# Encoder trunk on one core: x's two parts in one 512-column matmul, a new PSUM layout, and vectors fetched at other times

## The chip, the core and the metric

The kernel runs on one core of a Trainium2 chip. Its time is the device time of one execution in microseconds; a comparison uses the median over rounds. Engines are named as in the profile: PE is TensorE (PEld its weight loads), DVE is VectorE, ACT is ScalarE, POOL is GpSimd, and SP issues the DMAs.

## What is computed

Two layers work on x, 256 tokens of 1024 features in float32. Each layer has three steps, every one followed by a layer norm of `ALPHA*x + step`:

```python
x = layer_norm(ALPHA * x + 0.5 * swiglu(x, ffn1...))      # 1024 -> 2816 -> 1024
proj = x @ w_in                                             # u | gate_b | gate_c | h | q | k | v
y = concat(pool_mixer(u), gated_conv(gate_b, gate_c, h), neighbourhood_attention(q, k, v, rpb)) @ w_out
x = layer_norm(ALPHA * x + y)
x = layer_norm(ALPHA * x + 0.5 * swiglu(x, ffn2...))
# swiglu(x) = (silu(x @ w_gate) * (x @ w_up)) @ w_down
```

Attention has 8 heads of 64 columns on a grid of 4 rows by 64 columns, with a bias per head that is read from a small table, and a mask that keeps a query to 16 key columns.

## The kernel before

**Products.** Every operand is split exactly into a high and a low part that the matmul takes at full rate (`hi` is a cast on ACT, `lo = raw - hi` on DVE). A product is three matmuls: x's high part by the weight's high part, x's low part by the weight's high part, x's high part by the weight's low part.

**Weights.** Weights come in units of 512 KB by DMAs on SP's queue into four raw buffers. ACT (line 178) and DVE (line 179) split each unit into one of twelve pairs of slots. A unit is issued when a place is free, one per `pc.step`.

**Three ways of multiplying.** `x_stat` (lines 290 to 292) has x stationary and 512 weight columns moving: the first 512 gate and up columns, and v and u|gate_b. `w_stat` (lines 303 to 305) has 128 weight columns stationary and x's 256 tokens moving, so that its result comes out transposed: 256 columns of the weights make one group of two column tiles (`ft`) by eight chunks of the features (`kc`) by three matmuls. There are 36 pairs of such groups (gate and up) in the four feed-forward parts, and six groups (q0, k0, q1, k1, gate_c, h) in each mixer part. `r_stat` (lines 315 to 317) has transposed activations stationary and 512 columns of the down or output weights moving.

**PSUM.** Eight banks in two pools: four one-bank buffers `acc` for the accumulators (two token tiles by two halves) and the attention scores, four one-bank buffers `mm` for all else.

**Order of the work.** All five engines run their instructions in the order in which the program issues them. That order is set by the `Pacer`. Its clock advances with the matmuls issued (`MM512`, `MM256`); `pc.at(delay, ...)` puts a piece of work off until the first `pc.step` at which the clock has advanced by `delay`, and `pc.need(tag)` runs what is left of a tag. A step first runs the work that is due and then issues at most one weight unit. A `w_stat` group has four blocks of four `kc`, with a step after each of the first three and one more after the group's evacuation.

**Mixers.** After v and u|gate_b come q0, k0, q1, k1, gate_c, h, and then the output projection. The attention of four heads (`a0` from q0 and k0, `a1` from q1 and k1) goes in two calls of `attention`, two heads each, and four stages: `scores` (PE; DVE adds the bias and takes the maximum; ACT the exponentials), `normalise` (DVE, line 712), `transposed` (PE, line 721; ACT copies), `weighted` (PE, line 735; ACT and DVE write the output's two parts, lines 748 and 749). The delays between them are `A_S`, `A_NORM`, `A_TR`, `A_PV`. The convolution (`conv_mixer`, lines 662 to 668) follows the product h.

**Other vectors.** `load_gb` fetches the layer norm's two vectors, spread over the partitions, `GB_AT` after the part before has ended. `load_bias` fetches a bias (four DMAs, lines 572 and following) and adds the mask on POOL (line 579). The layer norm's `rs = (var + eps)^-0.5` is two POOL instructions (lines 342 and 343).

Of the kernel before, what the change touches and what calls it, by code (L numbers as in the profile page):

```python
# [16 lines left out]
P = 128  # L17
SEQ = 256
# [28 lines left out]
# units of the weights that go before the second token tile at the start, and where its transposes stand  # L47
X1_AT = 4
X1_TR = 3
# how long after its operands were ordered a step is issued, in microseconds of the tensor engine's work  # L50
LN_TR = (4.5, 7.2)
GB_AT = 14.0
# [5 lines left out]
A_NORM = 2.6  # L58
A_TR = 1.2
A_PV = 1.4  # L60
# about how long a product of the tensor engine takes: these pace the work of the other engines
MM512 = 0.218
MM256 = 0.1095


class Pacer:
    """Places work of the other engines, and the next weights, between groups of matrix products."""
# [53 lines left out]
def encoder_kernel(  # L121
# [18 lines left out]
    ps_acc = ctx.enter_context(tc.tile_pool(name="ps_acc", bufs=4, space=PSUM))  # L140
    ps_mm = ctx.enter_context(tc.tile_pool(name="ps_mm", bufs=4, space=PSUM))
# [14 lines left out]
    def mirrored(v):  # L156
        """The same view, its last axis run backwards."""
        dims = [list(d) for d in v.ap]
        step, n = dims[-1]
        dims[-1] = [-step, n]  # L160
        return bass.AP(tensor=v.tensor, offset=v.offset + (n - 1) * step, ap=dims)
# [4 lines left out]
    def bank(tag="mm"):  # L166
        pool = ps_mm if tag == "mm" else ps_acc
        return pool.tile([P, 512], F32, tag=tag, name=nm(tag))

# [88 lines left out]
    def new_xT():  # L258
        hi = xp.tile([P, KC, SEQ], F32R, tag="xhi", name=nm("xhi"))
        lo = xp.tile([P, KC, SEQ], F32R, tag="xlo", name=nm("xlo"))  # L260
        return hi, lo
# [32 lines left out]
    def w_stat(ps, key, xT):  # L294
        """256 columns of the weights against all tokens, transposed out."""
        for ft in range(2):
            c = slice(ft * P, (ft + 1) * P)
            for i in range(2):
                hi, lo = pc.get((*key, i))
                for j in range(4):  # L300
                    kc = i * 4 + j
                    o = ps[:, ft * SEQ : (ft + 1) * SEQ]
                    PE.matmul(o, hi[:, j, c], xT[0][:, kc, :], start=(kc == 0), stop=False)  # L303
                    PE.matmul(o, hi[:, j, c], xT[1][:, kc, :], start=False, stop=False)  # L304
                    PE.matmul(o, lo[:, j, c], xT[0][:, kc, :], start=False, stop=(kc == KC - 1))  # L305
                if ft == 1:
                    pc.free((*key, i))
                if ft == 0 or i == 0:
                    pc.step(12 * MM256)

    def r_stat(ps, key, act, t, n, first, last):
        """A chunk of transposed activations against half a row unit."""
        hi, lo = pc.get(key)
        ts = slice(t * P, (t + 1) * P)
        PE.matmul(ps, act[0][:, ts], hi[:, n, :], start=first, stop=False)  # L315
        PE.matmul(ps, act[1][:, ts], hi[:, n, :], start=False, stop=False)  # L316
        PE.matmul(ps, act[0][:, ts], lo[:, n, :], start=False, stop=last)  # L317

# [17 lines left out]
    def ln_rest(t, stats, store):  # L336
        g, b = gbs[-1]
        xt = xs[t]
        mv = sp.tile([P, 2], F32, tag="mv", name=nm("mv"))
        rs = sp.tile([P, 1], F32, tag="rs", name=nm("rs"))  # L340
        DVE.bn_aggr(mv, stats.rearrange("p a b -> p (a b)"))  # L341
        POOL.tensor_scalar(rs, mv[:, 1:2], EPS, None, ALU.add)  # L342
        POOL.tensor_tensor(rs, rs, half_t, ALU.pow)
        for h in range(2):
            DVE.scalar_tensor_tensor(xt[:, hs[h]], xt[:, hs[h]], mv[:, 0:1], g[:, hs[h]], ALU.subtract, ALU.mult)
        for c in hs:
            DVE.scalar_tensor_tensor(xt[:, c], xt[:, c], rs[:, 0:1], b[:, c], ALU.mult, ALU.add)
            if store:
                SP.dma_start(out[0, t * P : (t + 1) * P, c], xt[:, c])

    def finish(keys, act, acc, last_key, next_gb, store, stop):
        """The last products into acc, one token tile after the other, and the layer norm."""
        nT = None if store else new_xT()
        for t in range(NT):
            stats = sp.tile([P, 2, 6], F32, tag="stats", name=nm("stats"))
            # the first half of the columns is done early where something waits for the layer norm
# [42 lines left out]
    def ffn(key, xT, next_gb, stop, store=False):  # L399
# [17 lines left out]
        # first four column tiles with the token tiles apart  # L417
        gk, uk = (*key, "g", 0), (*key, "u", 0)
        if key == (0, 0):
# [9 lines left out]
            for k in (gk, uk):  # L429
                ps = [bank() for _ in range(NT)]  # L430
# [16 lines left out]
        else:  # L447
            for t in range(NT):
                pc.need(f"x{t}")
                gate = bank()  # L450
                x_stat(gate, gk, 512, t, xT, t == 1)
                sg = silu(gate)
                pc.step(6 * MM512)
                up = bank()
                x_stat(up, uk, 512, t, xT, t == 1)
                gated_transposed(t, (sg,), up)
                pc.step(6 * MM512)
# [6 lines left out]

        for p in range(2, NPAIR):
            gate = bank()
            w_stat(gate, (*key, "g", p), xT)
            sg = silu(gate)
            pc.step(12 * MM256)
            up = bank()  # L470
            w_stat(up, (*key, "u", p), xT)
            hT = hts[p] = new_h()
            hf = gated(up, sg).rearrange("p (a b) -> p a b", a=2)
            ACT.copy(hT[:, 0], hf)  # L474
            DVE.tensor_tensor(hT[:, 1], hf, f32(hT[:, 0]), ALU.subtract)
            pc.step(12 * MM256)
            pc.need("h")
            # the down projection runs behind
# [15 lines left out]
    consts = {}  # L494

    def setup():
# [8 lines left out]
        # additive mask of a query column block: its rows run with the column falling  # L505
# [38 lines left out]
        pc.at(30, "cw", columns)  # L544
        # the bias table, each line in the middle of a longer one
# [12 lines left out]
        # probabilities: the columns out of a block's reach stay zero  # L558
# [9 lines left out]
    def load_bias(l, q):  # L568
        n = 4 * ROWS
        rv = bp.tile([P, n, WIN], F32, tag="rbias", name=nm("rbias"))  # L570
        for r in range(ROWS):
            SP.dma_start(
                rv[r * QB : (r + 1) * QB, :, :],
                dram(consts["tabs"][r], (l * HEADS + 4 * q) * ROWS * TABW, [[1, QB], [TABW, n], [1, WIN]]),
            )
        bias = bp.tile([P, 2, n, KW], F32, tag="bias", name=nm("bias"))
# [6 lines left out]
        return bias  # L583

    def mixers(l, xT, next_gb, stop):
# [12 lines left out]
        biases = {0: load_bias(l, 0)}  # L598
# [31 lines left out]
        for t in range(NT):  # L630
            pc.need(f"x{t}")
            pv = bank()
# [3 lines left out]
            pu = bank()  # L636
# [16 lines left out]
        def proj(name):  # L653
            ps = bank()
            w_stat(ps, (*key, name), xT)
            return ps.rearrange("p (a b) -> p a b", a=2)
# [13 lines left out]
        def attention(j, qT, kT, q):  # L670
            """Two heads, in the upper and the lower half of the rows: one stage after the other."""
# [81 lines left out]
        def qk(q):  # L753
            pq = proj(f"q{q}")
            qT = hp.tile([P, 2, 2, P], F32, tag="qk", bufs=4, name=nm("qT"))
            for j in range(2):
                for b in range(2):
                    src = mirrored(pq[:, j, :].rearrange("p (r c) -> p r c", c=GRID)[:, :, b * QB : (b + 1) * QB])
                    ACT.mul(qT[:, j, b, :].rearrange("p (r c) -> p r c", c=QB), src, HD ** -0.5)
            pc.step(12 * MM256)  # L760
            pk = proj(f"k{q}")
            kT = hp.tile([P, 2, SEQ], F32, tag="qk", bufs=4, name=nm("kT"))
            ACT.copy(kT, pk)
# [4 lines left out]
            pc.step(12 * MM256)  # L768

        qk(0)  # L770
        pc.at(A_S + A_STEP + 2, "bias1", lambda: biases.update({1: load_bias(l, 1)}))
# [3 lines left out]
        ACT.copy(gc, p_)  # L775
        pc.step(12 * MM256)
        p_ = proj("h")
        z = ap_.tile([P, 2, SEQ + 2], F32, tag="a", name=nm("z"))
        POOL.memset(z[:, :, 0:1], 0.0)
        POOL.memset(z[:, :, SEQ + 1 :], 0.0)  # L780
        DVE.tensor_tensor(z[:, :, 1 : SEQ + 1], p_, gc, ALU.mult)
        conv_mixer(z)
        pc.step(12 * MM256)
# [8 lines left out]
        pc.need("ya")  # L792
        pc.need("a0")
# [9 lines left out]
        pc.need("a1")  # L803
# [42 lines left out]
```

## Time and profile before

| what | value |
|---|---|
| runs | 979.34, 980.66, 981.9 us; median 980.66 |
| profiled execution, span from first to last instruction | 979.4 us (no other time is given for it) |
| PE busy | 950.6 us, 97%, 6201 matmuls |
| PEld busy | 865.1 us, 88% |
| DVE busy | 580.3 us, 59% |
| ACT busy | 437.7 us, 45% |
| POOL busy | 65.6 us, 7% |
| moved by DMA | 178.95 MB, mean 183 GB/s |

A row of the profile's groups gives line, engine, operation, output and inputs, the count, the busy time with the mean of one instruction, and the idle time of the engine before them with what ended it. Timeline rows start with the time in the span and the duration. Matmuls overlap each other, so a matmul's duration is longer than the step from one start to the next, and a "busy" PE can still be slowed; the steps are what counts.

### The profile page before, as it was taken

What the parts mean: (1) busy time and instruction counts of PE and PEld (TensorE: products, weight loads), DVE (VectorE), ACT (ScalarE), POOL (GpSimd) and SP (SyncE); (2) the same over time, 40 slices, a digit from 0 to 9 for tenths busy, and PEclk for the clock granted to TensorE, in tenths of its full rate; (3) what the DMA queues carried; (4) which work ended last, traced back from release to release, by engine and by line L of the source; (5) the groups of instructions that cost most, each with busy time, mean ns of one, the idle gap of its engine ahead of it and who ended that gap; (6) DMA issues with size and microseconds to landing.
All of it is one profiled execution on the core that took longest, in us unless ns stands there. A gap on an engine that the chain in (4) does not pass through costs nothing.

```text
span 979.4 us, 15259 instructions
## 1 busy us (share of the span) xinstructions
PE 950.6 (97%) x6201; PEld 865.1 (88%) x6201; DVE 580.3 (59%) x670; ACT 437.7 (45%) x585; POOL 65.6 (7%) x118
## 2 busy tenths in 40 slices
PE   7999999998999999999999999999889999999996
PEld 5999999878888999999888999998688889999995
DVE  5755544676768644545676454548676776454525
ACT  6544434335734534434344444443465354344410
POOL 4000000024101000000000000002050000000001
PEclk9999999999999999999999999999989999999999
DMA  8887665568345866565468556664754377556601
GB/s 287 277 264 216 190 194 173 145 185 241 106 129 169 258 194 188 175 195 177 135 211 254 176 172 194 191 186 110 252 153 123 109 229 243 177 174 193 192 23 43
DMA packets 129077, 178.95 MB, mean 183 GB/s; under 512 B 14752, under 2 KB 100848, under 8 KB 129008
## 3 DMA queue, kind: packets, MB, share of 16 engines
q1 hardware_dynamic: 129008, 177.99, 59.3%
q8 instruction: 48, 0.79, 0.3%
q14 instruction: 21, 0.17, 0.0%
HBM read 176.84 MB, written 1.13 MB: 182 GB/s over the span
## 4 chain that ended last, share of the span: by engine, by line
PE 83%; DVE 7%; DMA 5%; issue 2%; ACT 1%; POOL 1%; SPq 1%; POOLq 0%; DVEq 0%; ACTq 0%
PE mm L303 16%; PE mm L304 16%; PE mm L305 16%; PE acc L315 9%; PE acc L316 9%; PE acc L317 9%; DMA raw<-in_w_in_dram 3%; DVE wlo L179 2%; PE mm L292 2%; PE mm L290 2%; PE mm L291 2%; ACT whi L178 1%; PE mm L721 1%; DMA raw<-in_ffn_w_down_dram 1%; DMA raw<-in_ffn_w_up_dram 1%
## 5 line engine op out<-in xcount | busy, mean ns | idle before, releaser
L179 DVE TENSOR_TENSOR wlo<-raw,whi 128x1024 fp32r<-128x1024 f32 (+1 forms) x321 | 390.0, 1231 | 303.1 <-ACT whi L178 302.0
L178 ACT CAST whi<-raw 128x1024 fp32r<-128x1024 f32 (+1 forms) x321 | 331.1, 1045 | 328.9 <-issue 131.2
L303 PE MATMUL mm<-xhi,whi 128*128 128x256 f32 x1344 | 384.0, 286 | 0.0
L304 PE MATMUL mm<-xlo,whi 128*128 128x256 f32 x1344 | 382.0, 284 | 0.0
L305 PE MATMUL mm<-xhi,wlo 128*128 128x256 f32 x1344 | 381.8, 284 | 0.0
L303 PEld LDWEIGHTS mm<-xhi,whi 128*128 128x128 f32 x1344 | 259.7, 193 | 3.0 <-issue 1.5
L304 PEld LDWEIGHTS mm<-xlo,whi 128*128 128x128 f32 x1344 | 259.6, 193 | 1.4
L305 PEld LDWEIGHTS mm<-xhi,wlo 128*128 128x128 f32 x1344 | 259.5, 193 | 0.0
L315 PE MATMUL acc<-whi,hT 128*128 128x512 f32 x352 | 137.9, 392 | 0.0
L316 PE MATMUL acc<-whi,hT 128*128 128x512 f32 x352 | 137.4, 390 | 0.0
L317 PE MATMUL acc<-wlo,hT 128*128 128x512 f32 x352 | 137.0, 389 | 0.0
L317 PEld LDWEIGHTS acc<-wlo,hT 128*128 128x128 f32 x352 | 66.1, 188 | 14.0
L291 PE MATMUL mm<-whi,xlo 128*128 128x512 f32 x192 | 75.3, 392 | 2.9 <-DVE xlo L271 2.9
L315 PEld LDWEIGHTS acc<-whi,hT 128*128 128x128 f32 x352 | 66.2, 188 | 12.7
L316 PEld LDWEIGHTS acc<-whi,hT 128*128 128x128 f32 x352 | 66.2, 188 | 12.3
L290 PE MATMUL mm<-whi,xhi 128*128 128x512 f32 x192 | 76.7, 399 | 0.4 <-ACT whi L178 0.4
L292 PE MATMUL mm<-wlo,xhi 128*128 128x512 f32 x192 | 75.2, 392 | 0.5 <-DVE wlo L179 0.5
L342 POOL TENSOR_SCALAR rs<-mv 128x1 f32<-128x1 f32 x12 | 9.4, 780 | 847.0 <-DVE mv L341 847.0
L474 ACT CAST hT<-hf 128x512 fp32r<-128x512 f32 x36 | 22.3, 620 | 75.2 <-DVE hf L396 75.2
L291 PEld LDWEIGHTS mm<-whi,xlo 128*128 128x128 f32 x192 | 36.4, 189 | 10.8 <-DVE xlo L271 3.8
L292 PEld LDWEIGHTS mm<-wlo,xhi 128*128 128x128 f32 x192 | 36.2, 188 | 8.9 <-DVE wlo L179 1.3
L290 PEld LDWEIGHTS mm<-whi,xhi 128*128 128x128 f32 x192 | 36.3, 189 | 8.2 <-ACT whi L178 1.3
(93 smaller groups left out, 556.9 us busy)
## 6 DMA issues: line engine op xcount, KB each, us to landing
raw<-in_ffn_w_up_dram SPq DMA_DIRECT2D x88, 512.0 KB, 4.7
raw<-in_ffn_w_down_dram SPq DMA_DIRECT2D x88, 512.0 KB, 4.1
raw<-in_ffn_w_gate_dram SPq DMA_DIRECT2D x87, 512.0 KB, 4.1
raw<-in_w_in_dram SPq DMA_DIRECT2D x40, 512.0 KB, 4.7
raw<-in_w_out_dram SPq DMA_DIRECT2D x16, 512.0 KB, 4.8
lng<-in_ln_g_dram SPq DMA_DIRECT2D x6, 512.0 KB, 6.8
lnb<-in_ln_b_dram SPq DMA_DIRECT2D x6, 512.0 KB, 8.3
rbias<-tab SPq DMA_DIRECT2D x16, 96.0 KB, 5.1
```

The source lines that it names most:

```text
L178: ACT.copy(hi, raw)
L179: DVE.tensor_tensor(lo, raw, f32(hi), ALU.subtract)
L290: PE.matmul(ps, xT[0][:, kc, ts], hi[:, j, :], start=(kc == 0), stop=False)
L291: PE.matmul(ps, xT[1][:, kc, ts], hi[:, j, :], start=False, stop=False)
L292: PE.matmul(ps, xT[0][:, kc, ts], lo[:, j, :], start=False, stop=(kc == KC - 1))
L303: PE.matmul(o, hi[:, j, c], xT[0][:, kc, :], start=(kc == 0), stop=False)
L304: PE.matmul(o, hi[:, j, c], xT[1][:, kc, :], start=False, stop=False)
L305: PE.matmul(o, lo[:, j, c], xT[0][:, kc, :], start=False, stop=(kc == KC - 1))
L315: PE.matmul(ps, act[0][:, ts], hi[:, n, :], start=first, stop=False)
L316: PE.matmul(ps, act[1][:, ts], hi[:, n, :], start=False, stop=False)
L317: PE.matmul(ps, act[0][:, ts], lo[:, n, :], start=False, stop=last)
L474: ACT.copy(hT[:, 0], hf)
```

## The change

- `xT` becomes one tile with both parts of x. In `w_stat` the two matmuls with the weight's high part become one with 512 moving columns (two runs of 256: high part, low part). Its result fills one bank: the first half takes the products with x's high part, the second those with x's low part. The third matmul adds into the first half.
- After each `w_stat` group, ACT copies the second half out of PSUM (`lower`), and DVE adds it to the first. Silu, the halving of up, and the product of the two then work on SBUF.
- PSUM: two buffers `mm` of two banks each, for `w_stat` and `x_stat`; four one-bank buffers `acc` for all else (accumulators, scores, transposes, attention output, pooling product).
- `GB_AT` is 45 rather than 14. The first bias of a mixer part is fetched and masked in the feed-forward part before (at pair 6), and the second is fetched there too and masked at `BIAS_AT`.
- `rs`'s addition of eps is a DVE instruction.
- `A_NORM` is 3.6 rather than 2.6, `A_TR` 2.2 rather than 1.2. `a1` is completed before the output projection rather than after its first two keys. The transpose of the convolution's taps comes in the first mixer part.
- Comments go.

```diff
-GB_AT = 14.0
+GB_AT = 45.0
-A_NORM = 2.6
-A_TR = 1.2
+A_NORM = 3.6
+A_TR = 2.2
+BIAS_AT = A_S + A_STEP + 3.0
-MM256 = 0.1095
+MM768 = 0.347
...
-    ps_acc = ctx.enter_context(tc.tile_pool(name="ps_acc", bufs=4, space=PSUM))
-    ps_mm = ctx.enter_context(tc.tile_pool(name="ps_mm", bufs=4, space=PSUM))
+    ps_one = ctx.enter_context(tc.tile_pool(name="ps_one", bufs=4, space=PSUM))
+    ps_two = ctx.enter_context(tc.tile_pool(name="ps_two", bufs=2, space=PSUM))
...
+    def bank(tag="acc"):
+        return ps_one.tile([P, 512], F32, tag="acc", name=nm(tag))
+    def banks():
+        return ps_two.tile([P, 2, 2, SEQ], F32, tag="mm", name=nm("mm"))
...
-        hi = xp.tile([P, KC, SEQ], F32R, tag="xhi", name=nm("xhi"))
-        lo = xp.tile([P, KC, SEQ], F32R, tag="xlo", name=nm("xlo"))
-        return hi, lo
+        both = xp.tile([P, 2, KC, SEQ], F32R, tag="xT", name=nm("xT"))
+        return both[:, 0], both[:, 1], both
...
-                    PE.matmul(o, hi[:, j, c], xT[0][:, kc, :], start=(kc == 0), stop=False)
-                    PE.matmul(o, hi[:, j, c], xT[1][:, kc, :], start=False, stop=False)
-                    PE.matmul(o, lo[:, j, c], xT[0][:, kc, :], start=False, stop=(kc == KC - 1))
+                    PE.matmul(ps[:, ft], hi[:, j, c], xT[2][:, :, kc, :], start=(kc == 0), stop=False, ...)
+                    PE.matmul(ps[:, ft, 0], lo[:, j, c], xT[0][:, kc, :], start=False, stop=(kc == KC - 1), ...)
...
+    def lower(ps, scale=1.0):
+        t = tp.tile([P, 2, SEQ], F32, tag="t", name=nm("lw"))
+        ACT.activation(t, ps[:, :, 1], AF.Copy, scale=scale)
+        return t
...
-        POOL.tensor_scalar(rs, mv[:, 1:2], EPS, None, ALU.add)
+        DVE.tensor_scalar(rs, mv[:, 1:2], EPS, None, ALU.add)
...
+        def bias_ahead():
+            ahead["bias"] = {0: add_mask(fetch_bias(key[0], 0))}
+            ahead["rv"] = fetch_bias(key[0], 1)
+            if key[1] == 0 and p == 6:
+                pc.at(0, "bias", bias_ahead)
...
-            gate = bank()
+            gate = banks()
             w_stat(gate, (*key, "g", p), xT)
-            sg = silu(gate)
-            pc.step(12 * MM256)
-            up = bank()
+            sg = lower(gate)
+            DVE.tensor_tensor(sg, gate[:, :, 0], sg, ALU.add)
+            ACT.activation(sg, sg, AF.Silu)
+            pc.step(4 * MM768)
+            up = banks()
             w_stat(up, (*key, "u", p), xT)
             hT = hts[p] = new_h()
-            hf = gated(up, sg).rearrange("p (a b) -> p a b", a=2)
+            hf = lower(up, 0.5)
+            DVE.scalar_tensor_tensor(hf, up[:, :, 0], 0.5, hf, ALU.mult, ALU.add)
+            DVE.tensor_tensor(hf, hf, sg, ALU.mult)
...
             pq = proj(f"q{q}")
+            ql = lower(pq, HD ** -0.5)
+            DVE.scalar_tensor_tensor(ql, pq[:, :, 0], HD ** -0.5, ql, ALU.mult, ALU.add)
-                    ACT.mul(qT..., src, HD ** -0.5)      # src from PSUM
+                    ACT.copy(qT..., src)                  # src from ql
...
-            ACT.copy(kT, pk)
+            kl = lower(pk)
+            DVE.tensor_tensor(kT, pk[:, :, 0], kl, ALU.add)
...
-        pc.at(A_S + A_STEP + 2, "bias1", lambda: biases.update({1: load_bias(l, 1)}))
+        pc.at(BIAS_AT, "bias1", lambda: biases.update({1: add_mask(rv1)}))
...
-        ACT.copy(gc, p_)
+        gl = lower(p_)
+        DVE.tensor_tensor(gc, p_[:, :, 0], gl, ALU.add)
...
-        DVE.tensor_tensor(z[:, :, 1 : SEQ + 1], p_, gc, ALU.mult)
+        hl = lower(p_)
+        DVE.tensor_tensor(hl, p_[:, :, 0], hl, ALU.add)
+        DVE.tensor_tensor(z[:, :, 1 : SEQ + 1], hl, gc, ALU.mult)
         conv_mixer(z)
...
-        pc.need("ya")
-        pc.need("a0")
+        for tag in ("ya", "a0", "a1"):
+            pc.need(tag)
         for k in keys[:2]:
...
-        pc.need("a1")
         return finish(keys[2:], act, acc, keys[-1], next_gb, False, stop)
```

More of the change, by code (lines that the diff above doesn't have):

```diff
@@ L164, in halves, with apart @@
         return [slice(i * n // 2, (i + 1) * n // 2) for i in range(2)]
-    def bank(tag="mm"):
-        pool = ps_mm if tag == "mm" else ps_acc
-        return pool.tile([P, 512], F32, tag=tag, name=nm(tag))
+    def bank(tag="acc"):
+        return ps_one.tile([P, 512], F32, tag="acc", name=nm(tag))
+    def banks():
+        return ps_two.tile([P, 2, 2, SEQ], F32, tag="mm", name=nm("mm"))
+    def apart(two):
+        return two.rearrange("p a b c -> p a (b c)")
     def unit_tiles(shape):
@@ L301, in w_stat @@
                     kc = i * 4 + j
[L302 to L305, printed above, removed]
+                    PE.matmul(
+                        ps[:, ft], hi[:, j, c], xT[2][:, :, kc, :],
+                        start=(kc == 0), stop=False, skip_group_check=True,
+                    )
+                    PE.matmul(
+                        ps[:, ft, 0], lo[:, j, c], xT[0][:, kc, :],
+                        start=False, stop=(kc == KC - 1), skip_group_check=True,
+                    )
                 if ft == 1:
@@ L428, in ffn @@
             res = []
-            for k in (gk, uk):
-                ps = [bank() for _ in range(NT)]
+            both = [apart(banks()) for _ in range(NT)]
+            for which, k in enumerate((gk, uk)):
+                ps = [b[:, which] for b in both]
                 seq = [(i, t) for i in range(4) for t in range(NT)]
@@ L449, in ffn @@
                 pc.need(f"x{t}")
-                gate = bank()
+                both = apart(banks())
+                gate, up = both[:, 0], both[:, 1]
                 x_stat(gate, gk, 512, t, xT, t == 1)
@@ L463, in act @@
             return [hts[f // 2][:, i, f % 2, :] for i in range(2)]
+        def bias_ahead():
+            ahead["bias"] = {0: add_mask(fetch_bias(key[0], 0))}
+            ahead["rv"] = fetch_bias(key[0], 1)
         for p in range(2, NPAIR):
-            gate = bank()
+            if key[1] == 0 and p == 6:
+                pc.at(0, "bias", bias_ahead)
+            gate = banks()
             w_stat(gate, (*key, "g", p), xT)
-            sg = silu(gate)
-            pc.step(12 * MM256)
-            up = bank()
+            sg = lower(gate)
+            DVE.tensor_tensor(sg, gate[:, :, 0], sg, ALU.add)
+            ACT.activation(sg, sg, AF.Silu)
+            pc.step(4 * MM768)
+            up = banks()
             w_stat(up, (*key, "u", p), xT)
             hT = hts[p] = new_h()
-            hf = gated(up, sg).rearrange("p (a b) -> p a b", a=2)
+            hf = lower(up, 0.5)
+            DVE.scalar_tensor_tensor(hf, up[:, :, 0], 0.5, hf, ALU.mult, ALU.add)
+            DVE.tensor_tensor(hf, hf, sg, ALU.mult)
             ACT.copy(hT[:, 0], hf)
             DVE.tensor_tensor(hT[:, 1], hf, f32(hT[:, 0]), ALU.subtract)
-            pc.step(12 * MM256)
+            pc.step(4 * MM768)
             pc.need("h")
@@ L542, in columns @@
             DVE.tensor_copy(cw, trp)
-        pc.at(30, "cw", columns)
+        consts["columns"] = columns
         tab = ap_.tile([P, 7 * TABW], F32, tag="a", name="tab")
@@ L565, in setup, with fetch_bias @@
         consts.update(icnt=icnt, mask=mask, pw=pw, cw=cw, tabs=tabs)
-    def load_bias(l, q):
+    def fetch_bias(l, q):
         n = 4 * ROWS
@@ L575, in load_bias, with add_mask @@
             )
+        return rv
+    def add_mask(rv):
+        n = 4 * ROWS
         bias = bp.tile([P, 2, n, KW], F32, tag="bias", name=nm("bias"))
@@ L583, in load_bias @@
         return bias
+    ahead = {}
     def mixers(l, xT, next_gb, stop):
@@ L597, in mixers @@
         POOL.memset(U[:, :, PADL + SEQ :], 0.0)
-        biases = {0: load_bias(l, 0)}
+        biases, rv1 = dict(ahead.pop("bias")), ahead.pop("rv")
+        if l == 0:
+            pc.at(POOL_AT - 4, "cw", consts["columns"])
         def pool_means():
@@ L631, in mixers @@
             pc.need(f"x{t}")
-            pv = bank()
+            both = apart(banks())
+            pv, pu = both[:, 0], both[:, 1]
             x_stat(pv, (*key, "v"), 512, t, xT, t == 1)
@@ L635, in mixers @@
             pc.step(6 * MM512)
-            pu = bank()
             x_stat(pu, (*key, "ug"), 512, t, xT, t == 1)
@@ L653, in proj @@
         def proj(name):
-            ps = bank()
+            ps = banks()
             w_stat(ps, (*key, name), xT)
-            return ps.rearrange("p (a b) -> p a b", a=2)
+            return ps
         def conv_mixer(z):
@@ L754, in qk @@
             pq = proj(f"q{q}")
+            ql = lower(pq, HD ** -0.5)
             qT = hp.tile([P, 2, 2, P], F32, tag="qk", bufs=4, name=nm("qT"))
+            DVE.scalar_tensor_tensor(ql, pq[:, :, 0], HD ** -0.5, ql, ALU.mult, ALU.add)
             for j in range(2):
                 for b in range(2):
-                    src = mirrored(pq[:, j, :].rearrange("p (r c) -> p r c", c=GRID)[:, :, b * QB : (b + 1) * QB])
-                    ACT.mul(qT[:, j, b, :].rearrange("p (r c) -> p r c", c=QB), src, HD ** -0.5)
-            pc.step(12 * MM256)
+                    src = mirrored(ql[:, j, :].rearrange("p (r c) -> p r c", c=GRID)[:, :, b * QB : (b + 1) * QB])
+                    ACT.copy(qT[:, j, b, :].rearrange("p (r c) -> p r c", c=QB), src)
+            pc.step(4 * MM768)
             pk = proj(f"k{q}")
             kT = hp.tile([P, 2, SEQ], F32, tag="qk", bufs=4, name=nm("kT"))
-            ACT.copy(kT, pk)
+            kl = lower(pk)
+            DVE.tensor_tensor(kT, pk[:, :, 0], kl, ALU.add)
             first = attention(0, qT, kT, q)
@@ L767, in qk @@
             pc.at(A_S + A_STEP, f"a{q}", second)
-            pc.step(12 * MM256)
+            pc.step(4 * MM768)
         qk(0)
-        pc.at(A_S + A_STEP + 2, "bias1", lambda: biases.update({1: load_bias(l, 1)}))
+        pc.at(BIAS_AT, "bias1", lambda: biases.update({1: add_mask(rv1)}))
         qk(1)
@@ L774, in mixers @@
         gc = ap_.tile([P, 2, SEQ], F32, tag="a", name=nm("gc"))
-        ACT.copy(gc, p_)
-        pc.step(12 * MM256)
+        gl = lower(p_)
+        DVE.tensor_tensor(gc, p_[:, :, 0], gl, ALU.add)
+        pc.step(4 * MM768)
         p_ = proj("h")
+        hl = lower(p_)
         z = ap_.tile([P, 2, SEQ + 2], F32, tag="a", name=nm("z"))
@@ L780, in mixers @@
         POOL.memset(z[:, :, SEQ + 1 :], 0.0)
-        DVE.tensor_tensor(z[:, :, 1 : SEQ + 1], p_, gc, ALU.mult)
+        DVE.tensor_tensor(hl, p_[:, :, 0], hl, ALU.add)
+        DVE.tensor_tensor(z[:, :, 1 : SEQ + 1], hl, gc, ALU.mult)
         conv_mixer(z)
-        pc.step(12 * MM256)
+        pc.step(4 * MM768)
         acc = [[None, None], [None, None]]
```

## The prediction

> **What bounds the kernel now.** I read the share of each engine, the groups by line, PE's timeline, and then the waits around PE's idle stretches. PE is busy 97% of the span, and lines 303 to 305 hold the largest part:
>
> ```profile
> PE 950.6 (97%) x6201; PEld 865.1 (88%) x6201; DVE 580.3 (59%) x670; ACT 437.7 (45%) x585; POOL 65.6 (7%) x118
> PE mm L303 16%; PE mm L304 16%; PE mm L305 16%; PE acc L315 9%; PE acc L316 9%; PE acc L317 9%; DMA raw<-in_w_in_dram 3%; DVE wlo L179 2%; PE mm L292 2%; PE mm L290 2%; PE mm L291 2%; ACT whi L178 1%; PE mm L721 1%; DMA raw<-in_ffn_w_down_dram 1%; DMA raw<-in_ffn_w_up_dram 1%
> ...
> L303 PE MATMUL mm<-xhi,whi 128*128 128x256 f32 x1344 | 384.0, 286 | 0.0
> ```
>
> What counts is the step from start to start:
>
> ```profile
> 101.19 0.28 PE L305 MATMUL mm<-xhi,wlo 128*128 128x256 f32 x1
> 101.31 0.40 PE L315 MATMUL acc<-whi,hT 128*128 128x512 f32 x1
> ...
> 106.55 0.39 PE L317 MATMUL acc<-wlo,hT 128*128 128x512 f32 x1
> 106.77 0.28 PE L303 MATMUL mm<-xhi,whi 128*128 128x256 f32 x1
> ...
> 242.97 0.28 PE L303 MATMUL mm<-xhi,whi 128*128 128x256 f32 x1
> ...
> 246.56 0.28 PE L303 MATMUL mm<-xhi,whi 128*128 128x256 f32 x1
> ```
>
> Between the two 512-column ends lie 24 matmuls: (106.77 - 101.31) / 24 = 0.2275 us each, the last of them followed by a 256-column one (0.22). The last two rows are ten triples of 256 columns apart: 0.359 us a triple, 0.120 a matmul, also where a 512-column one follows (101.19 to 101.31). So 512 columns cost less than two times 256: about 13 ns per matmul do not depend on the columns.
>
> PE's idle time lies mostly in the two mixer parts:
>
> ```profile
> 202.43 4.10 DVE L347 SCALAR_TENSOR_TENSOR x<-x,rs,lnb 128x512 f32<-128x512 f32 x2 [0.47 <-POOL rs L343]
> 202.46 3.52 POOL L579 TENSOR_TENSOR bias<-rbias,mask 128x640 f32<-128x640 f32 x2
> 295.26 1.42 DVE L347 SCALAR_TENSOR_TENSOR x<-x,rs,lnb 128x512 f32<-128x512 f32 x2 [0.46 <-POOL rs L343]
> 211.73 0.50 PE L291 MATMUL mm<-whi,xlo 128*128 128x512 f32 x1 [1.47 <-DVE xlo L271]
> 209.25 0.50 SPq L325 DMA_DIRECT2D lng<-in_ln_g_dram  x1
> 220.09 1.05 ACT L178 CAST whi<-raw 128x1024 fp32r<-128x1024 f32 x1 [4.19 <-DMA raw<-in_w_in_dram]
> 227.76 1.11 PE L644 MATMUL mm<-ident,un 128*128 128x128 f32 x4 [3.17 <-ACT un L639]
> 707.73 0.66 PE L644 MATMUL mm<-ident,un 128*128 128x128 f32 x4 [3.05 <-ACT un L639]
> 228.00:232.00 4.00, 4.00 (x24) 4.00 (x24) 2.04 (x3) 1.32 (x2) 2.22 (x2) 0.64 0.85 312
> 708.00:712.00 4.00, 4.00 (x24) 4.00 (x23) 2.01 (x3) 1.32 (x2) 1.37 (x1) 0.59 0.91 334
> 247.96 0.30 PE L721 MATMUL mm<-ident,pz 128*128 128x128 f32 x1 [0.87 <-DVE pz L712]
> 249.44 1.79 PE L721 MATMUL mm<-ident,pz 128*128 128x128 f32 x11 [1.18 <-DVE pz L712]
> 728.56 0.30 PE L721 MATMUL mm<-ident,pz 128*128 128x128 f32 x1 [1.39 <-DVE pz L712]
> 730.04 2.18 PE L721 MATMUL mm<-ident,pz 128*128 128x128 f32 x9 [1.18 <-DVE pz L712]
> 731.00:736.00 5.00, 5.00 (x25) 5.00 (x24) 2.79 (x7) 3.29 (x5) 0.00 (x0) 0.50 0.36 102
> ```
>
> In order: a layer norm's DVE step took 2.05 us while POOL masked a bias, 0.71 without, and PE waited 1.47 for the x behind it; the layer norm vectors went out ahead of weights, ACT waited 4.19 us for a weight, and PE over 3 us for ACT's copy behind it; PE waited for the softmax. In the three windows the last but two numbers show the granted clock: 0.5 to 0.64 after idle stretches of some 3 us.
>
> **The change, part by part.**
>
> *The merged matmul.* A triple (0.359) becomes 0.2275 + 0.120 = 0.3475. By 1344: 15.5 us; with the steps that follow one another without rounding (0.360 against 0.347) 17.5. I take **-17**. No row has a moving operand in two runs; the bounds are one matmul (0.2275) and two (0.240), the second giving nothing. I take the first, since both runs are of 256 contiguous columns.
>
> The Trainium skill's page "TensorE: Matmul & The Clock Gate" (section "Back-to-back issue gap") gives N/2.4 + 2.5 ns for a gap: by it the triple would go from 327 to 325 ns, and the change would save 3.4 us. The trace's 120 and 227.5 ns contradict so small a fixed part.
>
> *The evacuation.* Per group one ACT copy and one DVE addition more (84 groups), and for up a DVE product; 0.59 and 0.69 us each by the rows below. Gate: copy, addition, silu end some 2.5 us after the group, and its two banks are needed again after up's 5.6 us. hT's chain (0.6 + 2 x 0.69 + 0.62 + 0.69) meets its use one pair later. **Nothing** there; without that cover it would be 84 x 1.6 = 134 us. In the mixers it does not stay free (below).
>
> *Vectors fetched elsewhere.* The wait for un goes (6.2 us in both parts; I keep 0.5 each for the weights' own rate): **-5.2**, and the slowed clock after it, 4 x 0.36 + 4 x 0.41 = **-3.1**. The bias mask no longer lies on the layer norm: **-3.0** (1.47 twice). What is moved: two 512 KB DMAs to 45 us, among weights that have twelve places of lead; and in the feed-forward part two fetches of a bias, the second of which holds SP until POOL has masked the first (5.1 us landing and two masks of 1.7 each, 8.5 us). SP normally waits for buffers, so weights late by that much cost ACT a wait, not PE: 0, at most 2 us a layer.
>
> *eps on DVE.* Layer norms wait 0.46 for POOL less; only the last one ends the kernel: **-0.3**. The taps' transpose: 0.
>
> *The softmax.* The waits before (0.87 + 1.18 + 1.39 + 1.18) go, **-4.6**, and half the clock in five to six us, **-3.0**. In their place comes the new order. Rows for it:
>
> ```profile
> rbias<-tab SPq DMA_DIRECT2D x16, 96.0 KB, 5.1
> L396 DVE SCALAR_TENSOR_TENSOR hf<-mm,sg 128x512 f32<-128x512 f32 x44 | 30.0, 685 | 13.7 <-PE mm L305 12.5 <-PE mm L292 1.2
> L391 ACT ACTIVATE sg<-mm 128x512 f32<-128x512 f32 x44 | 26.2, 597 | 21.5 <-PE mm L305 18.3 <-PE mm L292 3.2
> L712 DVE TENSOR_SCALAR pz<-pz,sm 128x160 f32<-128x160 f32 x32 | 12.6, 435 | 0.6
> 241.23 1.36 PE L686 MATMUL acc<-kT,qT 64*128 64x160 f32 x16
> 242.84 0.48 DVE L695 TENSOR_TENSOR Sb<-acc,bias 128x320 f32<-128x320 f32 x1
> 248.44 0.18 ACT L700 ACTIVATION_READ_ACCUMULATOR pz<-Sb,mx 128x1 f32 x1
> L721 PE MATMUL mm<-ident,pz x16: 272/279/329, 267.6 to 269.9; 128*128 128x128 f32 x16
> L735 PE MATMUL mm<-PT,v x16: 379/379/430, 273.0 to 274.6; 128*64 128x256 f32 x16
> ```
>
> A step is now 4 x 0.347 = 1.39 us, so the stages fall on steps 2, 5, 7 and 9 after k is ordered (they fell on 2, 4, 5 and 7). On step 5 `normalise` stands behind a weight's split and, for a0, behind q1's addition. Let K be the end of k0's matmuls: 239.8 before (scores at 241.23 follow a block of 1.4 later). The bias addition started at K + 3.0 and the exponentials ended at K + 8.8. With kT's addition: K + 9.4. Then cast 1.05, split 1.23, addition 0.69, and four heads' scaling at 0.63 each: first head ready at K + 13.0, last at 14.9. PE reaches the transposes at K + 6 x 1.39 + 1.36 = 9.7, idles 3.3, and ends at 15.4 instead of 12.1: **+3.3**. For a1, k1's addition, the output of a0 and a split hold the bias addition until K + 5.2; the same chain gives the first head at 13.4, the last at 15.3. PE arrives at K + 1.8 + 1.36 + 8.3 = 11.5: **+1.9**.
>
> *The output projection.* a1's `weighted` falls on step 9, which comes behind `conv_mixer` on ACT and DVE, and its two results take two of the four `acc` banks, which the third and fourth accumulator need.
>
> ```profile
> 274.14 0.27 ACT L748 CAST yT<-mm 128x128 fp32r<-128x128 f32 x1 [1.84 <-PE mm L735]
> ...
> 275.92 0.29 DVE L749 TENSOR_TENSOR yT<-mm,yT 128x128 fp32r<-128x128 f32 x1 [0.33 <-ACT yT L748]
> ...
> 277.87 0.40 PE L315 MATMUL acc<-whi,yT 128*128 128x512 f32 x1
> ...
> 278.73 0.68 DVE L781 TENSOR_TENSOR z<-mm,gc 128x512 f32<-128x512 f32 x1
> ...
> 283.04 0.62 ACT L667 CAST yT<-cs 128x512 fp32r<-128x512 f32 x1 [5.49 <-DVE cs L665]
> ```
>
> h ended at E = 277.9; z came 0.85 later, the cast of y 4.3 after z. With h's addition the cast ends at E + 0.85 + 0.69 + 4.3 + 0.62 = 6.45, DVE's low part at 7.2, and the first result's four readings (a pair of results took 274.14 to 276.21) at 8.1. PE has issued `weighted` (1.8) and two accumulators (6 x 0.2275) by E + 3.15: **+4.95**. Bounds: 0 if the banks were free, 6.4 if the fourth accumulator waits as long.
>
> *Clock.* An idle 5 us costs some 3.4 us at half speed, 1.7, in both parts; the transposes' idle 3.3 does so more often than not, the 1.9 rarely: **+6** in all.
>
> *Sum:* -17 - 5.2 - 3.1 - 3.0 - 0.3 - 4.6 - 3.0 = -36.2; 2 x (3.3 + 1.9 + 4.95) + 6 = +26.3; together -9.9 on a span of 979.4. The median is 980.66, 1.3 above the span: **971 us**.
>
> **Rivals.**
>
> *Two runs cost two matmuls.* Place: every w_stat triple. At 0.240 instead of 0.2275 the -17 is gone: 988, slower. It decides from 9.5 ns on (12.8 us / 1344). For: no such operand in the trace. Against: nothing else in a matmul's step depends on where its columns lie in these rows. 6%. The skill page's formula would, in this sum, give 985; the rows speak against it: 3%.
>
> *The evacuation beside POOL.* Where POOL works, DVE took 2.05 for 0.71; the convolution's 4.3 us so slowed is 12, and the wait at the output projection 8 longer in both parts: 987. It decides from 6.4 a part. POOL has only short work there: 7%.
>
> *The banks are free.* If a1's results are read before the accumulators want them, 9.9 and their clock go: 958. Against: the order just counted. 20%. If the softmax is hidden too, 945: 6%.
>
> *Gains and new waits cancel* (each new wait 1 to 2 us longer): 978 to 983.6, 13%.
>
> **How the numbers follow.** The forecast (962 to 977.7) has 45%. Range 951 to 986: it leaves out 945, 987 and 988 (0.19). About 0.3%, 2.9 us, can be told from no change: faster 0.45 + 0.20 + 0.06 = 0.71, same 0.13, slower 0.06 + 0.03 + 0.07 = 0.16.
>
> **What would show it.** Line 303's successor at steps of 0.227 and 0.120; no wait for un and none of L291 for xlo in the mixers; the transposes of pz waiting for DVE some 3 and 2 us; the third accumulator of the output projection 5 us late behind yT, the granted clock low after it. Wrong if the 512-column step is 0.24, or if PE runs through the mixers without these waits.

## The result, and the profile after

The changed kernel takes 998.63 us (997.76 to 999.25) against 981.28 before, a ratio of 1.018 with an interval of 1.0165 to 1.0198: slower by some 17 us, where 971 was forecast. The page of the profiled execution (999.25 us, span 997.5):

```profile
span 997.5 us, 12731 instructions
PE 952.5 (95%) x4857; PEld 794.7 (80%) x4857; DVE 629.5 (63%) x766; ACT 484.5 (49%) x663; POOL 58.5 (6%) x106
...
L308 PE MATMUL mm<-xT,whi 128*128 128x512 f32 x1344 | 479.9, 401 | 4.8 <-DVE hf L412 4.8
L312 PE MATMUL mm<-xT,wlo 128*128 128x256 f32 x1344 | 378.0, 281 | 0.0
L296 PE MATMUL mm<-whi,xT 128*128 128x512 f32 x192 | 80.1, 417 | 12.0 <-ACT sg L407 8.9
```

PE runs 1344 matmuls fewer than before and is busy for longer. Line 296 (the first matmul of `x_stat`, line 290 before) has 12 us of idle time in front of it; it had 0.4. PE's list of waits (engine and line, what it waited for, us in total, times, longest) says the same of the whole kernel (some rows):

```profile
PE acc L331 <- DVE yT L784: 9.3, 2, 4.6
PE mm L296 <- ACT sg L407: 8.9, 6, 2.0
...
PE mm L308 <- DVE hf L412: 4.8, 1, 4.8
PE acc L756 <- DVE pz L747: 4.6, 4, 1.4
PE mm L296 <- ACT v L670: 2.7, 4, 0.7
PE acc L721 <- DVE kT L801: 1.1, 2, 0.5
...
PE acc L679 <- ACT un L674: 0.4, 1, 0.4
```

and of the kernel before:

```profile
PE mm L644 <- ACT un L639: 6.2, 2, 3.2
...
PE mm L721 <- DVE pz L712: 4.6, 4, 1.4
PE mm L291 <- DVE xlo L271: 2.9, 2, 1.5
```

The waits for un and xlo are gone, as forecast, and the output projection's wait (first row) has come, as forecast. The rows for sg, v and hf were not forecast: 16.4 us. Timeline rows and two windows of them (the window's last three numbers are the granted clock, DMA's share and GB/s):

```profile
39.39 0.63 PE L308 MATMUL mm<-xT,whi 128*128 128x512 f32 x1 [4.75 <-DVE hf L412]
318.70 0.50 PE L296 MATMUL mm<-whi,xT 128*128 128x512 f32 x1 [2.03 <-ACT sg L407]
...
39.50:43.00 3.50, 3.50 (x11) 2.95 (x12) 2.70 (x3) 1.96 (x3) 0.00 (x0) 0.51 0.92 315
319.50:322.90 3.40, 3.40 (x9) 2.64 (x8) 1.44 (x2) 0.08 (x1) 0.00 (x0) 0.51 0.97 304
```

Line 296 writes the second of `x_stat`'s two results (up; u and gate_b). In the new layout that result is the other bank of the tile in which the first (gate; v) stands, and PE now waits until ACT has read the first one. At 39.39 the first `w_stat` group waits for the buffer in which up was still to be read by DVE. Behind the waits at 39.39 and 318.70 the granted clock was 0.51 for 3.4 us; whether the waits alone cause that is taken up with the experiments.

The merged matmul gave half of what was counted. Rows of a triple, and the start of line 308 eleven triples on:

```profile
99.77 0.40 PE L308 MATMUL mm<-xT,whi 128*128 128x512 f32 x1
100.00 0.28 PE L312 MATMUL mm<-xT,wlo 128*128 128x256 f32 x1
100.12 0.40 PE L308 MATMUL mm<-xT,whi 128*128 128x512 f32 x1
...
103.65 0.40 PE L308 MATMUL mm<-xT,whi 128*128 128x512 f32 x1
```

From 99.77 to 103.65 it is 3.88 / 11 = 0.353 us a triple, against 0.359 before and 0.3475 forecast. Within a triple, the step after the 512 columns has a median of 0.236 in this trace, the step after the 256 one of 0.117.

### The profile page after: what moved, and what is told of

Its sections match the earlier page's. It is cut to its first block, busy times and chain, and to the rows that moved or that the text cites. A ratio compares the mean times of both kernels' runs of the same rounds, so it can differ in the third digit from the quotient of the medians.

```text
span 997.5 us, 12731 instructions
## 1 busy us (share of the span) xinstructions
PE 952.5 (95%) x4857; PEld 794.7 (80%) x4857; DVE 629.5 (63%) x766; ACT 484.5 (49%) x663; POOL 58.5 (6%) x106
## 4 chain that ended last, share of the span: by engine, by line
PE 86%; DVE 5%; ACT 4%; DMA 3%; issue 1%; SPq 0%; DVEq 0%; ACTq 0%
PE mm L308 29%; PE mm L312 15%; PE acc L331 10%; PE acc L333 10%; PE acc L332 10%; PE mm L296 4%; PE mm L298 3%; PE mm L297 3%; DVE wlo L186 2%; ACT whi L185 2%; DMA raw<-in_w_in_dram 1%; PE acc L274 1%; ACT pz L735 1%; DMA raw<-in_ffn_w_gate_dram 1%; PE acc L756 1%
## 5 line engine op out<-in xcount | busy, mean ns | idle before, releaser
L308 PE MATMUL mm<-xT,whi 128*128 128x512 f32 x1344 | 479.9, 401 | 4.8 <-DVE hf L412 4.8
L312 PE MATMUL mm<-xT,wlo 128*128 128x256 f32 x1344 | 378.0, 281 | 0.0
L308 PEld LDWEIGHTS mm<-xT,whi 128*128 128x128 f32 x1344 | 253.2, 188 | 68.4 <-issue 6.6
L312 PEld LDWEIGHTS mm<-xT,wlo 128*128 128x128 f32 x1344 | 254.6, 189 | 1.3
L296 PE MATMUL mm<-whi,xT 128*128 128x512 f32 x192 | 80.1, 417 | 12.0 <-ACT sg L407 8.9
L298 PE MATMUL mm<-wlo,xT 128*128 128x512 f32 x192 | 77.4, 403 | 0.0
L297 PE MATMUL mm<-whi,xT 128*128 128x512 f32 x192 | 77.4, 403 | 0.0
L332 PEld LDWEIGHTS acc<-whi,hT 128*128 128x128 f32 x352 | 66.2, 188 | 12.7
L324 ACT ACTIVATE lw<-mm 128x512 f32<-128x512 f32 x84 | 50.2, 598 | 36.5 <-PE mm L312 36.4
L296 PEld LDWEIGHTS mm<-whi,xT 128*128 128x128 f32 x192 | 37.3, 194 | 24.5 <-ACT sg L407 11.4
L298 PEld LDWEIGHTS mm<-wlo,xT 128*128 128x128 f32 x192 | 37.5, 195 | 9.1 <-DVE wlo L186 1.0
L297 PEld LDWEIGHTS mm<-whi,xT 128*128 128x128 f32 x192 | 37.7, 196 | 7.2
L502 DVE TENSOR_TENSOR hT<-lw,hT 128x512 fp32r<-128x512 f32 x36 | 24.9, 693 | 24.7 <-ACT hT L501 24.7
```

The source lines that it names most:

```text
L296: PE.matmul(ps, xT[0][:, kc, ts], hi[:, j, :], start=(kc == 0), stop=False)
L297: PE.matmul(ps, xT[1][:, kc, ts], hi[:, j, :], start=False, stop=False)
L298: PE.matmul(ps, xT[0][:, kc, ts], lo[:, j, :], start=False, stop=(kc == KC - 1))
L308: PE.matmul(ps[:, ft], hi[:, j, c], xT[2][:, :, kc, :], start=(kc == 0), stop=False, skip_group_check=True,)
L312: PE.matmul(ps[:, ft, 0], lo[:, j, c], xT[0][:, kc, :], start=False, stop=(kc == KC - 1), skip_group_check=True,)
L324: ACT.activation(t, ps[:, :, 1], AF.Copy, scale=scale)
```

## The experiments

The runs came in three groups of four kernels, in the order below, each group beside new runs of the kernel before (981.28 beside the changed kernel itself), which took 980.4, 980.3 and 981.9 us (medians). A few microseconds between kernels of different groups are uncertain: in the third group the runs of the kernel before lay between 975.4 and 984.0 us.

**Own banks for `x_stat`'s results.**

```diff
-                both = apart(banks())
-                gate, up = both[:, 0], both[:, 1]
+                gate = bank()
                 x_stat(gate, gk, 512, t, xT, t == 1)
...
+                up = bank()
                 x_stat(up, uk, 512, t, xT, t == 1)
# the same for v and u|gate_b, and for the first part's gate and up
```

> The changed kernel, but x_stat's two results (gate and up, v and u|gate_b) each take a one-bank buffer of their own instead of halves of one two-bank tile. Theory A (the matmuls of the second result wait until the first one's reader on ACT is done, because both stand in one tile; the trace of the changed kernel shows eight such waits before line 296 of 0.84 to 2.19 us, 12.7 in all, one of 4.92 before the first w_stat group, and three windows of 3.4 us at half clock behind them, 1.7 each): these waits go, 12.7 + 4.9 + 5.1 = 22.7 us, so about 976. Rival B (ACT is late there anyway, and any layout would wait): within 3 us of the changed kernel's 998.6.

Measured: 976.37 us, 22.3 less than the changed kernel, 0.996 of the kernel before (0.9943 to 0.9978). PE's waits:

```profile
PE acc L331 <- DVE yT L783: 9.3, 2, 4.6
...
PE acc L755 <- DVE pz L746: 5.1, 4, 2.0
PE acc L678 <- ACT un L673: 2.0, 2, 1.5
PE acc L424 <- DVE hf L412: 1.7, 2, 1.3
```

The rows for sg and v are gone, and 1.7 us are left of the 4.8 for hf (now in front of its transposes). The wait for un rose from 0.4 to 2.0. The time fell by the expected amount, though not term by term: the expectation's eight waits of 12.7 us are ten of 11.6 in the list above, and some 2 of the 22 us between the two profiled executions arise at the very start, ahead of the first of these waits (last section). Some 20 us are left for the edit. That settles the largest part: the shared tile, not a late ACT.

**Contiguous columns.**

```diff
-        both = xp.tile([P, 2, KC, SEQ], F32R, tag="xT", name=nm("xT"))
-        return both[:, 0], both[:, 1], both
+        both = xp.tile([P, KC, 2, SEQ], F32R, tag="xT", name=nm("xT"))
+        return both[:, :, 0], both[:, :, 1], both.rearrange("p k a t -> p k (a t)")
```

> The changed kernel with xT laid out so that a chunk's high and low columns stand side by side: the 512 moving columns of line 308 are one contiguous run instead of two runs of 256 that lie 8 KB apart. Theory A (the second run costs the 9 ns by which the step after line 308, median 236 ns, exceeds the 227 of a contiguous 512-column matmul): the step becomes 227, and 1344 x 0.0065 (the triple 353.5 against 347) gives 8.7 us, so about 990. Rival B (the 9 ns come from alternating 512 and 256 columns, or from PSUM): the step stays near 236 and the time within 3 us of 998.6.

Measured: 997.91 us (996.19 to 1000.94). The triple stays at 0.353:

```profile
99.67 0.40 PE L308 MATMUL mm<-xT,whi 128*128 128x512 f32 x1
...
103.56 0.40 PE L308 MATMUL mm<-xT,whi 128*128 128x512 f32 x1
```

So the two runs are not what costs it, and the forecast's rival on them (988 us, the nearest of the forecast's times to the result) is wrong too.

**The attention's output one step earlier.**

```diff
-A_PV = 1.4
+A_PV = 1.38
```

> The changed kernel with A_PV 1.38 instead of 1.40, so that the attention's last stage falls one step earlier, ahead of the convolution on ACT and DVE. Theory A (the output projection's third accumulator waits 4.80 us in each mixer part for banks that hold the attention's output, which ACT and DVE read only after the convolution; 6.8 us at half clock follow each): 2 x 4.8 + 2 x 3.4 = 16 us less, about 982. Rival B (the wait moves to another operand of the output projection, or to the transposes): at most 5 us less, 994 or more.

Measured: 979.9 us, 18.7 less than the changed kernel. PE's waits no longer have a row for yT; those for pz fell from 4.6 to 2.7, and kT's rose from 1.1 to 2.6:

```profile
PE mm L296 <- ACT sg L407: 8.9, 6, 2.0
...
PE acc L756 <- DVE pz L747: 2.7, 4, 1.1
...
PE acc L721 <- DVE kT L801: 2.6, 4, 0.8
```

A delay of 1.4 against a step of 1.388 had put the stage two steps later rather than one.

The gain is more than the 16 us expected, and the trace shows a reason. The waits for sg in front of line 296 are all still there, yet the clock behind the one of 2.03 us, and behind its like in the second layer, was now full (last three numbers):

```profile
309.71 0.50 PE L296 MATMUL mm<-whi,xT 128*128 128x512 f32 x1 [2.03 <-ACT sg L407]
310.40:313.80 3.40, 3.40 (x21) 2.89 (x20) 1.55 (x2) 0.78 (x3) 0.00 (x0) 1.00 0.97 286
788.60:792.00 3.40, 3.40 (x21) 2.89 (x20) 1.52 (x3) 0.78 (x3) 0.00 (x0) 1.00 0.89 300
```

These two stretches at half clock, at 319.5 and its like in the second layer, thus needed both the wait for sg and the output projection's stall before it: in the profiled executions they go with either edit, while the kernel with contiguous columns, which has both the wait and the stall, has them too. The one at 39.5 is still there (38.5 in this kernel) and belongs to the shared tile alone.

**All three.**

> The three edits together: one-bank buffers for x_stat, contiguous columns, the attention's output one step earlier. If the three costs are separate they add: 998.6 - 22.7 - 8.7 - 16 = 951. If they hide one another (a wait taken away uncovers the next, in the softmax of the mixers), 960 to 970.

Measured: 961.87 us, 0.981 of before (0.979 to 0.983). The three gains alone add to 41.7 us; together they are 36.8. The two stretches at half clock that go with either edit, some 1.7 us each, are counted twice in the first sum, which makes 3.4 of the difference of 4.9; 0.7 more is what the contiguous columns seemed to bring alone, with no change in their steps. Own banks bring 22.3 us alone and 18.0 where the output is already early (979.9 to 961.87). Between the start and the last few microseconds no stretch at half clock is left; pz and kT still cost 3.7 and 2.1 us of waits.

**The third matmul into the other half of the bank, and 512 columns in both matmuls.**

```diff
-                        ps[:, ft, 0], lo[:, j, c], xT[0][:, kc, :],
+                        ps[:, ft, 1], lo[:, j, c], xT[0][:, kc, :],     # first kernel
+                        ps[:, ft], lo[:, j, c], xT[2][:, kc, :],        # second kernel
```

> All three edits, and the third matmul of w_stat (256 columns) adds into the second half of the bank, with the products of x's low part, rather than the first (the halves are added afterwards anyway). Theory A (the step of 236 instead of 227 after the 512-column matmul comes from adding into the columns that were written first): steps 227 and 120, 1344 x 0.0065 = 8.7 us less than the kernel with all three edits (961.9), 953. Rival B (it comes from alternating 512 and 256 columns, or from the operand): step 236, within 2 us of 962.

> All three edits, and the second matmul of w_stat also moves 512 columns (it adds the product of both low parts, which the kernel leaves out), so that no 256-column matmul is left there. Theory A (alternating sizes cost the 9 ns): every step 227, a triple's place taken by 2 x 227 = 454 ns instead of 353.5, 1344 x 0.1005 = 135 us more, about 1097. Rival B (w_stat's operands or its bank cost it): the step stays near 236, 2 x 236 = 472, about 1121.

Measured: 960.4 us for the first, no change to tell; eleven of its triples took 3.87 us (starts of line 308 at 106.04 and 109.91), 0.352 each. The second took 1082.97 us (one run), and its steps are as theory A has them:

```profile
103.93 0.39 PE L308 MATMUL mm<-xT,whi 128*128 128x512 f32 x1
...
108.91 0.39 PE L308 MATMUL mm<-xT,whi 128*128 128x512 f32 x1
```

4.98 / 11 = 0.453, two steps of 0.2264. The time is 14 us under theory A's 1097. Some 6 of these are the waits for pz and kT, of which this kernel has none; the rest is not accounted for. The operands and the bank are those of the kernel with all three edits, so the 6 ns a triple appear only where 512 and 256 columns are mixed.

**Three matmuls of 256 again.** `w_stat` as before the change, with its direct evacuation, and all else as with all three edits.

> All three edits, but w_stat goes back to three matmuls of 256 columns, and the copy and addition after each group are gone. Theory A (the merge is worth its steps, 360 against 353.5 ns, and its evacuation is hidden): 8.7 us more than 961.9, 970 to 971. Rival B (the added work on ACT and DVE costs as much as the steps bring, through the waits for the softmax in the mixers): within 2 us of 962 or below.

Measured: 964.77 us, 2.9 more than with all three edits and 4.4 more than the kernel with the other half of the bank, which was run in the same group: between the theories. The steps are worth 1344 x 6.5 ns = 8.7 us; half of it or more goes back. PE's waits without the merge:

```profile
PE acc L757 <- DVE pz L748: 2.1, 4, 1.1
```

No wait for kT is left (2.1 with the merge), and 2.1 for pz rather than 3.7: the copy and addition after each group are not hidden in the mixers. These 3.7 us are what the waits show of the amount that goes back; the rest is not accounted for.

**The softmax's scaling one step earlier.**

```diff
-A_NORM = 3.6
-A_TR = 2.2
+A_NORM = 2.7
+A_TR = 4.0
```

> All three edits, with A_NORM 2.7 and A_TR 4.0: the softmax's scaling falls one step earlier, ahead of the next weight's split on DVE, and the transposes stay on their step. Theory A (the transposes wait for pz, 1.40 and 0.34, 0.63, 1.64 and 0.34, 0.62, because the scaling stands behind that split and the addition for q1): these 5 us go, about 957. Rival B (the exponentials on ACT end too late in any order): within 2 us of 962.

Measured: 965.68 us (961.66 to 968.9), not better than 961.87. The scaling did go ahead of the split and was complete sooner, but PE then waited for a bank (waits in a stretch of the first mixer part, and rows of POOL and DVE there):

```profile
PE acc L755 <- ACT ya L657: 3.5, 1, 3.5
...
ACT qT L795 <- DVE lw L791: 3.0, 1, 3.0
...
239.15 3.10 POOL L609 TENSOR_TENSOR bias<-rbias,mask 128x640 f32<-128x640 f32 x2 [4.32 <-DVE Sb L729]
239.70 2.72 DVE L746 TENSOR_SCALAR pz<-pz,sm 128x160 f32<-128x160 f32 x2
242.52 0.52 DVE L746 TENSOR_SCALAR pz<-pz,sm 128x160 f32<-128x160 f32 x2
```

The transposes need four banks, one of which held the pooling product; ACT read it only behind its copies of q, which waited for DVE's addition. DVE was late with that in part because the scaling now ran beside POOL's masking of the second bias: the first head's took 2.72 us there, 0.52 once POOL was done. The second layer has the same (2.71). Neither theory had that wait, and how the order would do without POOL beside it was not tried.

**Order by size; the layer norm vectors early again; the merge in the feed-forward parts alone; and the first with the third.**

```diff
# by size: in a block of w_stat, first the four matmuls of 512 columns, then the four of 256
                 for j in range(4):
                     PE.matmul(ps[:, ft], hi[:, j, c], xT[2][:, kc, :], ...)
+                for j in range(4):
                     PE.matmul(ps[:, ft, 0], lo[:, j, c], xT[0][:, kc, :], ...)
# vectors early
-GB_AT = 45.0
+GB_AT = 14.0
# feed-forward alone: proj() calls a w_stat of three 256-column matmuls, read out as before the change
```

> All three edits, and in each block of w_stat the four 512-column matmuls come first and then the four of 256, so that the size changes twice in eight matmuls rather than after each. Theory A (a change of size costs the 6.5 ns a triple): three quarters of 1344 x 6.5 ns = 6.6 us less than 961.9, 955. Rival B (the cost belongs to each 512-column matmul beside others of 256, or to the loads, whatever the order): the sum of a triple's steps stays near 353, 962.

> All three edits with GB_AT back at 14: the layer norm's vectors go out among the first weights of each part again. Theory A (as in the kernel before, ACT then waits for a weight and PE for the copy un in both mixer parts, 3.2 us and 1.5 at half clock each; 0.9 and 1.1 are there now): 2 x (3.2 + 1.5) - 2 = 7.4 us more, 969. Rival B (the bias fetched earlier frees the queue enough): within 2 us of 962.

> All three edits, but the six groups of each mixer part go back to three matmuls of 256 columns, without the copy and addition; the feed-forward parts keep the merge. Theory A (in the feed-forward parts the evacuation is hidden and the merge worth its steps; in the mixers the added work on ACT and DVE returns as waits of the scores and transposes): the mixers lose 192 x 6.5 ns = 1.2 us and gain the waits for kT (0.67, 0.93, 0.25, 0.93) and some of those for pz (4.6 against 2.8 with no merge): 958. Rival B (the merge gives its steps everywhere, and the 2.9 us by which the kernel with three matmuls throughout was slower are all it is worth): 962 to 964.

> The last and the first of these together: the merge in the feed-forward parts alone, its matmuls in order of size. If both gains hold and add: 1152 x 6.5 ns x 3/4 = 5.6 us less than 958, 952. If order by size does nothing: 958.

Measured: 958.8 (by size), 965.73 (vectors early, 962.2 to 966.15), 958.02 (feed-forward alone) and 954.58 (both; 0.973 of before, 0.970 to 0.976). The last lies between the two times that its expectation gives.

By size gains 3.1 (against 961.87 of the first group) where a cost per change of size would have given 6.6. Merged timeline rows of a block, the start and the busy time of the four matmuls:

```profile
100.41 0.64 PE L314 MATMUL mm<-xT,wlo 128*128 128x256 f32 x4
100.89 1.09 PE L308 MATMUL mm<-xT,whi 128*128 128x512 f32 x4
101.81 0.63 PE L314 MATMUL mm<-xT,wlo 128*128 128x256 f32 x4
```

Four of 512 take 0.92, 0.230 each, and four of 256 take 0.48: 1.40 for four triples, 0.350 each. Better than 0.353, short of 0.347. What the mixing costs is thus not the change of size alone, and it stays open.

With the vectors early the wait for un came back in part (PE's waits):

```profile
PE acc L678 <- ACT un L673: 3.7, 2, 2.5
```

3.7 us against 1.7 with the vectors late; the time is 3.9 higher, but the two kernels were not run side by side, and the runs of this kernel spread as much. The bias fetched earlier took the rest of that wait, or the vectors cost less than counted: not told apart.

With the merge in the feed-forward parts alone there is no wait for kT, and pz's fell to 2.2, as theory A has it:

```profile
PE acc L771 <- DVE pz L762: 2.2, 4, 1.4
```

Both together is the fastest kernel of this study.

## Why the prediction was wrong

**The step that failed** is the one on the evacuation: it asked for every `w_stat` group whether its two banks were read out before they were needed again, found cover of 5.6 us, and costed the layout at nothing. It did not ask it for `x_stat`, where the two results that follow each other directly had been put into one tile. There is no cover there: PE goes from the last matmul of the first to the first of the second, and ACT's reading begins only at that moment. Measured: 16.4 us of waits and a stretch of 3.4 us at half clock (some 1.7 lost), with two more such stretches that needed the output projection's stall as well; by experiment 22.3 us, of which some 2 may be the start, and 18.0 where the output was early.

**The merged matmul** was right in mechanism and mis-sized: 0.353 rather than 0.3475 us a triple, 8.7 us rather than 17. The step of 512 columns was taken from rows with other 512s around them; beside 256s it is 0.236, which nearly meets the forecast's own sign of being wrong (0.24), while the 256 behind it takes 0.117. This was not the operand in two runs, which the prediction had as its rival and bound. Its weighing of the fixed part against the Trainium skill's formula on the page "TensorE: Matmul & The Clock Gate" (section "Back-to-back issue gap") came out for the trace: with 256 columns alone the step was 120 ns and with 512 alone 226, where N/2.4 + 2.5 gives 109 and 216. That section gives the formula for a matmul by itself and not for a stream, which the prediction does not say.

**What held.** The wait for un (6.2 to 0.4; forecast 5.2 less) and for xlo (2.9 to none; 3.0), and the stretches at half clock behind un and the softmax are gone. The output projection: 4.63 us of wait in the first mixer part where 4.95 was counted, for the reason counted. DVE and ACT around it, and the clock after it:

```profile
280.71 0.69 DVE L822 TENSOR_TENSOR z<-lw,gc 128x512 f32<-128x512 f32 x1
285.05 0.62 ACT L702 CAST yT<-cs 128x512 fp32r<-128x512 f32 x1 [5.15 <-DVE cs L700]
286.31 0.28 DVE L784 TENSOR_TENSOR yT<-acc,yT 128x128 fp32r<-128x128 f32 x1
287.36 0.77 PE L331 MATMUL acc<-whi,yT 128*128 128x512 f32 x1 [4.63 <-DVE yT L784]
287.40:292.10 4.70, 4.70 (x11) 3.77 (x12) 2.68 (x4) 2.25 (x3) 0.00 (x0) 0.50 0.19 39
```

The cast came 4.34 after z (4.3 counted), and half the clock lasted some 5 us from PE's start, where 3.4 was counted. From the output projection's first matmul to the next part's first it took 30.0 and 30.5 us in the two layers (281.07 to 311.07, 767.96 to 798.50), rather than 22.7 in both: 15.1 more, where 2 x 4.95 and 3.4 for the clock, 13.3, was counted.

**The softmax** was too dear: waits of 4.6 for pz and 1.1 for kT, where 2 x (3.3 + 1.9) = 10.4 was counted, and no half clock behind them, where 2.6 of the 6 was for it: 7.3 less in all. In the first mixer part PE waited 1.16 us for the first head, not 3.3:

```profile
251.33 1.03 PE L654 MATMUL acc<-pT,pw 128*128 128x256 f32 x4
254.91 1.92 PE L756 MATMUL acc<-ident,pz 128*128 128x128 f32 x12 [1.16 <-DVE pz L747]
```

The head was ready some 11 us after k0's matmuls (243.8) rather than 13.0, and PE had the pooling product, which the forecast does not have there, ahead of the transposes.

**The clock.** The prediction reads half clock as what follows idle stretches of some 3 us. Its third window, at 731, follows waits of 1.39 and 1.18 us, and in the runs one and the same wait of 2.03 us was followed by half clock in the changed kernel and by the full clock where the output projection had not stalled before it. What decides it beyond that, the runs do not show.

**The sum** corrected: 971 + 8.3 (merge) + 20 to 22 (shared tile) + 1.8 (output projection) - 7.3 (softmax) = 994 to 996; measured 998.6. Some 2.3 us of what is left lie at the start (below).

## What to carry to other kernels

When buffers are regrouped, go through every user of the new tile and ask who writes its second part while its first is read; two results that follow each other on one engine belong in tiles of their own, as the kernel before had them. A delay in a hand-made schedule should stand clear of a multiple of its step: 1.40 against 1.388 cost 18.7 us here, the stretches at half clock included. A merge on the busiest engine is worth its steps only where the engines that must undo it have time: kept in the feed-forward parts, dropped in the mixers, ordered by size, together with the three edits, it gives 954.6 us, 2.7% under the kernel before.

## What the runs showed of the hardware

A 512-column matmul's step was 0.2264 us among others of 512 columns, and a 512 with a 256 took 0.353 together although the 256 alone takes 0.120: some 6 ns more than the parts (353 against 226 + 120), whether the operand was contiguous or not and whichever half of the bank was written.

Half clock did not follow from the length of the last wait alone: behind the same wait of 2.03 us it was 0.51 in the changed kernel and 1.00 in the kernel with the attention's output one step earlier.

Two scalings on DVE took 2.72 us beside POOL's masking and 0.52 without it.

At the start PE ran at half rate for a different time in each profiled execution. Among 512-column matmuls the step was 0.43 us at 13.1 in the changed kernel (first three rows) and 0.23 at 11.8 in the kernel before (last two):

```profile
9.00:15.60 6.60, 6.48 (x14) 4.11 (x14) 4.03 (x4) 3.15 (x3) 2.39 (x6) 1.00 0.96 337
13.12 0.63 PE L298 MATMUL mm<-wlo,xT 128*128 128x512 f32 x1
13.55 0.63 PE L296 MATMUL mm<-whi,xT 128*128 128x512 f32 x1
...
11.75 0.40 PE L291 MATMUL mm<-whi,xlo 128*128 128x512 f32 x1
11.98 0.39 PE L292 MATMUL mm<-wlo,xhi 128*128 128x512 f32 x1
```

The window has 1.00 for the clock all the same, but the trace's record of the granted clock begins only at 15.65 us in the changed kernel and at 8.99 in the kernel before, and the steps are short from about there on. In the profiled executions of this study that record begins between 7.2 and 15.65 us. The same eight transposes of x start at 15.91 us in the changed kernel, 13.61 before and 13.66 with own banks, so some 2.3 us of a difference between two executions can lie there; what decides it was not tried.
